# First block of a streaming-encoder layer: x's rows for the norm are loaded two steps sooner into their own memory, and the products of the first weights change order

## The chip, the cores and the metric

The kernel runs on one NeuronCore of a Trainium2 chip. The time is device microseconds of one execution. The runs of the kernel before took 1817.17, 1819.08 and 1819.1 us, median 1819.08 us.

The engines have short names here: PE is TensorE (matmuls; PEld its weight loads), DVE is VectorE, ACT is ScalarE, POOL is GpSimd, and SP is SyncE, which here only issues DMAs. Each engine works through its instructions in order and waits on semaphores.

## The reference, cut to what matters

One layer of an encoder on 256 rows of 2048 numbers: half a gated feed-forward block, a mixer (a state-space part S5 beside attention), a second half feed-forward block, and a gated embedding. The change touches the first feed-forward block and moves preparation of S5 that runs beside it.

```python
x = x + 0.5 * swiglu(rms_norm(x, ffn1_norm[i]), ffn1_w_gate[i], ffn1_w_up[i], ffn1_w_down[i])

def rms_norm(x, gain):
    y = x * lax.rsqrt(jnp.mean(x * x, axis=-1, keepdims=True) + EPS)
    return y * gain

def swiglu(h, w_gate, w_up, w_down):
    return (jax.nn.silu(h @ w_gate) * (h @ w_up)) @ w_down
```

## The kernel before, in words

**Products.** Every matrix product of float32 is split in three: a tensor is cast to a high part (`whi`, `nhi`) by ACT (L181 for weights, L281 or L193 for x), and DVE subtracts that from the source to get the low part (`wlo`, `nlo`; L184, L286, L195). PE adds up high x high (L344), low input x high weight (L345) and high input x low weight (L338). For PE the stationary side is the input and the moving side the weight, 512 columns wide.

**Tiling.** The 256 rows are two tiles of 128 (`t` = 0, 1). The hidden width is cut into blocks of 512 columns (`f`). For each block `gemm_block` (L352) runs over the 2048 input columns in four quarters of 512; a quarter is one DMA of 1 MB into a raw weight buffer (`raw`, five of them, L327 and L328), and is worked in two halves, each 12 matmuls: 2 input rows of 128, 2 row tiles, 3 products. A half is called a half step here; after each, `step()` advances all generators that run beside (`put_off(n, fn)` runs `fn` after n more of these steps). There are four pairs of `whi` and `wlo`, so a cast waits until PE has released the pair four half steps back. The first three blocks of the first feed-forward block take their gate and up products with `gemm_block`, first gate (8 half steps), then up (8 half steps).

**First block.** The first two quarters of the gate product (`first_quarters`, L255) come in small pieces so that PE can start early: four pieces `in_head` that hold x's first columns beside the weights, then x's next columns (`in_turned`) and weights of the second quarter. The inputs are multiplied by the norm's gain but not by the root: since the root is one number per row, it is applied later, at the silu (L720, `scale=xn.rs(t)`) and where gate and up meet (L741). It is computed from sums of squares of x's rows (`squares`, L445 to L453; ACT squares a 128 x 512 piece and sums along the row, L447), from rows that are loaded for this alone (`load_x`, L155 to L157, eight DMAs of 0.26 MB). In the kernel before these rows lie in two of the five raw weight buffers, which `place_x` (L141) takes for the whole of x from the start.

**Accumulators.** Four PSUM banks of 512 columns (`acc`). Gate of a block takes two, up two. The gate product of the second block therefore needs the banks of the first block's gate product, and can start only once the silu has read them.

**Order.** The program is written in steps, but the framework orders the instructions of each engine by its own planning, except where `pin` or `tc.issue_after(ins)` fixes a place. All loads of weights, of x and of the preparation's constants stand in SP's one queue. A DMA there waits for the landing of the DMA eight before it, and for the release of its buffer.

**Beside it** runs the preparation of S5 (`s5_prep`, L834): many small operations of DVE, constants made by ACT, and tables that go to DRAM and back (`rot`, written at L993; `bc` and `bt`, loaded at L1011 and L1012; `coef`, loaded by POOL at L1016). `bc` is used by ACT at L1038 and by DVE at L1032. The finished hidden blocks are turned by DVE (L218), two at a time, and moved into place by small DMAs (`hT`, L231).

Of the kernel before, what the change touches and what calls it, by code (L numbers as in the profile page):

```python
# [9 lines left out]
F32 = mybir.dt.float32  # L10
# [6 lines left out]
P = 128  # L17
# [16 lines left out]
def layer_kernel(ctx: ExitStack, tc: tile.TileContext, a: dict, shapes: dict, out: bass.AP):  # L34
# [60 lines left out]
    def start(g):  # L95
        beside.append(g)
        return g
# [30 lines left out]
    def make_masks():  # L128


        u = com("h")[:, :P]
        nc.sync.dma_start(u, a["not_ahead"])
        nc.scalar.activation(tri_r, u, AF.Copy, scale=-1.0)
        nc.scalar.activation(late_r, u, AF.Copy, scale=-(2.0 ** 100))
        nc.scalar.copy(ident_r, ident)
        nc.scalar.activation(all_r, ones, AF.Copy, scale=-1.0)


    xt = [[], []]
# [1 line left out]
    def place_x():  # L141
        for t in range(TT):
            x = wp.tile([P, ND, NB], F32, tag="raw", name=uid("x"), bufs=5)
            xt[t][:] = [x[:, n, :] for n in range(ND)]
# [4 lines left out]
            for t in range(TT):  # L149
                nc.gpsimd.dma_start(xt[t][n], rows[t * P : (t + 1) * P, n * NB : (n + 1) * NB])  # L150

    place_x()
    scr_x = dramp.tile([T, D], F32, name="scr_x")

    def load_x(n):  # L155
        for t in range(TT):
            nc.sync.dma_start(xt[t][n], a["x"][0, t * P : (t + 1) * P, n * NB : (n + 1) * NB])  # L157

    def load_turned(n):
# [13 lines left out]
        return gains[:, c0 + k : c0 + k + n]  # L173


    rests = []

    def split(hi, lo, src, scale=None, pinned=False):

        if scale is None:  # L180
            copy = nc.scalar.copy(hi, src)  # L181
            if pinned:
                pin(copy)
            rest = nc.vector.tensor_tensor(out=lo, in0=src, in1=hi.bitcast(F32), op=ALU.subtract)  # L184
            rests.append(rest.ins)
            return copy.ins, rest.ins
        else:
            split_each(hi.unsqueeze(1), lo.unsqueeze(1), src.unsqueeze(1), [scale])
# [142 lines left out]
    def gemm_half(ps, half, ts, start, stop, cols=slice(0, NB), in_turn=False):  # L331

        (ahi, alo), (h, hi, lo) = half

        def rest(j):
            for t in ts:
                lh = ahi[:, 2 * h + j, t * P : (t + 1) * P]
                nc.tensor.matmul(ps[t], lhsT=lh, rhs=lo[:, j, cols], start=False, stop=stop and j == 1)  # L338

        for j in range(2):  # L340
            for t in ts:
                lh = ahi[:, 2 * h + j, t * P : (t + 1) * P]
                ll = alo[:, 2 * h + j, t * P : (t + 1) * P]
                nc.tensor.matmul(ps[t], lhsT=lh, rhs=hi[:, j, cols], start=start and j == 0, stop=False)  # L344
                nc.tensor.matmul(ps[t], lhsT=ll, rhs=hi[:, j, cols], start=False, stop=False)  # L345
            if in_turn:
                rest(j)
        if not in_turn:
            for j in range(2):
                rest(j)  # L350
# [275 lines left out]
    def ffn(i, xn, nxt, bg=None):  # L626
# [26 lines left out]
        for f in range(NF):  # L653
# [69 lines left out]
            if f == 0:  # L723
                warm_up(8)
                first = first_quarters(wg, xn)
                put_off(6, next, prep)
            pg = gemm_block(xn, wg, f * NB, KD, first)
            sg = com("sg")
            if f == 0:
                for n in range(ND):  # L730
                    put_off(n, load_x, n)
                    put_off(n + 2, xn.squares, n)
                put_off(6, gate)
            else:
                gate()
            pu = gemm_block(xn, wu, f * NB, KD)
            if prep and f == 0:
                start(prep)
            hh = com("h")
            for t in range(TT):  # L740
# [93 lines left out]
    def s5_prep(pools):  # L834
        base = pools.enter_context(phase("prep"))
        par = get(base, "par", 3 * NR)
        nc.sync.dma_start(par, a["ssm_par"])
        yield
        make_masks()
# [985 lines left out]
```

## Time and profile before

| what | us |
|---|---|
| median of three runs | 1819.08 |
| the profiled execution | 1819.03 |
| its span, from the first to the last instruction | 1817.1 |
| PE busy in the span | 1807.7 |
| DVE busy | 1574.8 |
| ACT busy | 1065.7 |
| POOL busy | 104.5 |
| PE busy in the first 140 us | 135.55 |
| DVE busy in the first 140 us | 119.28 |

The span is read from the profiled execution; the 1.9 us beside it are the execution's time ahead of and behind the first and the last instruction. A row of a timeline reads: start in us from the span's start, duration, engine, line, operation, what it writes and reads, count; behind it in brackets how long the engine had stood idle and what ended the wait. A row of a windows view reads: the stretch, its length, then the busy time and number of instructions that PE, PEld, DVE, ACT and POOL have in it, the mean granted clock of PE as a share of full speed, the share of the DMA engines' time, and GB/s. Busy PE time counts matmuls that overlap as one.

### The profile page before, as it was taken

To read this page: it belongs to the slowest core of one execution; us is meant where nothing else is said; L and a number is where in the kernel's file an instruction comes from. 1 tells how busy PE (TensorE), PEld (TensorE's weight loads), DVE (VectorE), ACT (ScalarE), POOL (GpSimd) and SP (SyncE) were. 2 spreads that over 40 slices of the span, in tenths; PEclk is the share of its full clock that TensorE was granted. 3 is DMA by queue.
4 is the path that set the end of the run, shared out by engine and by line. 5 is a ranking of instruction groups with operands and counts; after the bars stand their busy time and mean duration, and the time that the engine had idled before them with its cause. 6 is when DMAs were issued, how large, how long until landed. Compare 5 with 4: busy or idle time off the path is not lost.

```text
span 1817.1 us, 24209 instructions
## 1 busy us (share of the span) xinstructions
PE 1807.7 (99%) x8914; PEld 1498.9 (82%) x8914; DVE 1574.8 (87%) x1840; ACT 1065.7 (59%) x1240; POOL 104.5 (6%) x160
## 2 busy tenths in 40 slices
PE   9999999999999999999999999999999999999998
PEld 7788888888888888888898888888888888888887
DVE  8978889999998896687567899999999999889875
ACT  7445456655565665365685566555565556566654
POOL 0020100000000001110021000000000010000000
PEclk9999999999999999999999999999999999999999
DMA  8699877677876667674636787777767786666663
GB/s 331 262 270 315 246 247 232 232 251 235 264 248 229 198 232 251 192 255 163 220 129 218 237 299 218 265 261 249 233 231 235 242 276 239 224 208 221 201 245 128
DMA packets 107799, 428.41 MB, mean 236 GB/s; under 512 B 24512, under 2 KB 48352, under 8 KB 65280
## 3 DMA queue, kind: packets, MB, share of 16 engines
q1 hardware_dynamic: 96832, 391.15, 61.2%
q0 software_dynamic: 10560, 35.40, 9.0%
q8 instruction: 70, 1.15, 0.2%
q14 instruction: 49, 0.40, 0.1%
q10 hardware_dynamic: 288, 0.31, 0.1%
HBM read 372.41 MB, written 10.88 MB: 211 GB/s over the span
## 4 chain that ended last, share of the span: by engine, by line
PE 95%; DVE 1%; DMA 0%; issue 0%; ACT 0%; DVEq 0%; ACTq 0%
PE acc L344 16%; PE acc L345 16%; PE acc L338 15%; PE aux L345 7%; PE aux L344 7%; PE aux L338 7%; PE acc L526 5%; PE acc L529 5%; PE acc L527 5%; PE aux L527 3%; PE aux L529 3%; PE aux L526 3%; PE aux L1233 0%; PE acc L1484 0%; PE acc L1489 0%; PE acc L1480 0%
## 5 line engine op out<-in xcount | busy, mean ns | idle before, releaser
L184 DVE TENSOR_TENSOR wlo<-raw,whi 128x1024 fp32r<-128x1024 f32 x478 | 578.8, 1224 | 127.4 <-ACT whi L181 122.0
L181 ACT CAST whi<-raw 128x1024 fp32r<-128x1024 f32 x478 | 496.1, 1050 | 297.7 <-PE acc L345 183.7
L344 PE MATMUL acc<-whi,nhi 128*128 128x512 f32 x908 | 357.5, 394 | 3.4 <-ACT sg L720 2.3
L345 PE MATMUL acc<-whi,nlo 128*128 128x512 f32 x908 | 355.0, 391 | 0.0
L338 PE MATMUL acc<-wlo,nhi 128*128 128x512 f32 x908 | 253.2, 390 | 0.1
L184 DVE TENSOR_TENSOR slo<-raw,shi 128x1024 fp32r<-128x1024 f32 x186 | 226.6, 1218 | 16.0 <-ACT shi L181 15.2
L181 ACT CAST shi<-raw 128x1024 fp32r<-128x1024 f32 x186 | 195.2, 1050 | 65.3 <-DMA raw<-in_ffn_w_down 22.2
L344 PEld LDWEIGHTS acc<-whi,nhi 128*128 128x128 f32 x908 | 171.2, 189 | 41.2 <-ACT sg L720 2.7
L338 PEld LDWEIGHTS acc<-wlo,nhi 128*128 128x128 f32 x908 | 170.8, 188 | 36.0 <-DVE wlo L184 0.5
L345 PEld LDWEIGHTS acc<-whi,nlo 128*128 128x128 f32 x908 | 171.3, 189 | 34.6
L181 ACT CAST whi<-sum 128x1024 fp32r<-128x1024 f32 x79 | 83.3, 1054 | 157.5 <-DVE sum L533 138.4
L181 ACT CAST shi<-sum 128x1024 fp32r<-128x1024 f32 x59 | 62.2, 1054 | 101.6 <-DVE sum L533 96.1
L533 DVE TENSOR_TENSOR sum<-sum,raw 128x1024 f32<-128x1024 f32 x92 | 112.3, 1221 | 0.9
L184 DVE TENSOR_TENSOR wlo<-sum,whi 128x1024 fp32r<-128x1024 f32 x79 | 96.4, 1222 | 5.0 <-ACT whi L181 4.3
L594 POOL DMA_DIRECT2D raw<-raw x44 | 38.2, 868 | 1031.8 <-DVE sum L533 697.4
L344 PE MATMUL aux<-whi,nhi 128*128 128x512 f32 x220 | 85.8, 390 | 0.0
L345 PE MATMUL aux<-whi,nlo 128*128 128x512 f32 x220 | 85.7, 390 | 0.0
L184 DVE TENSOR_TENSOR slo<-sum,shi 128x1024 fp32r<-128x1024 f32 x59 | 72.1, 1222 | 1.1 <-ACT shi L181 0.5
L338 PE MATMUL aux<-wlo,nhi 128*128 128x512 f32 x220 | 67.8, 390 | 0.0
L533 DVE TENSOR_TENSOR sum<-raw,raw 128x1024 f32<-128x1024 f32 x46 | 56.1, 1220 | 7.2 <-DMA raw<-in_ffn_w_up 3.5
L345 PE MATMUL acc<-whi,hlo 128*128 128x512 f32 x156 | 60.8, 390 | 0.0
L344 PE MATMUL acc<-whi,hhi 128*128 128x512 f32 x156 | 60.7, 389 | 0.0
(393 smaller groups left out, 3410.3 us busy)
## 6 DMA issues: line engine op xcount, KB each, us to landing
raw<-in_ffn_w_up SPq DMA_DIRECT2D x88, 1024.0 KB, 5.7
raw<-in_ffn_w_down SPq DMA_DIRECT2D x88, 1024.0 KB, 4.9
raw<-in_ffn_w_gate SPq DMA_DIRECT2D x86, 1024.0 KB, 7.0
raw<-in_w_in SPq DMA_DIRECT2D x32, 1024.0 KB, 5.1
raw<-raw POOLq DMA_DIRECT2D x46, 512.0 KB, 5.5
raw<-in_w_out SPq DMA_DIRECT2D x16, 1024.0 KB, 4.9
raw<-in_w_ple_gate SPq DMA_DIRECT2D x16, 1024.0 KB, 5.1
hT<-mid SPq DMA_DIRECT2D x160, 64.0 KB, 4.7
```

Of the source, the lines that this page charges most:

```text
L181: copy = nc.scalar.copy(hi, src)
L184: rest = nc.vector.tensor_tensor(out=lo, in0=src, in1=hi.bitcast(F32), op=ALU.subtract)
L338: nc.tensor.matmul(ps[t], lhsT=lh, rhs=lo[:, j, cols], start=False, stop=stop and j == 1)
L344: nc.tensor.matmul(ps[t], lhsT=lh, rhs=hi[:, j, cols], start=start and j == 0, stop=False)
L345: nc.tensor.matmul(ps[t], lhsT=ll, rhs=hi[:, j, cols], start=False, stop=False)
L526: nc.tensor.matmul(ps, lhsT=lh[j], rhs=hi[:, j], start=begin and j == 0, stop=False)
L527: nc.tensor.matmul(ps, lhsT=ll[j], rhs=hi[:, j], start=False, stop=False)
L529: nc.tensor.matmul(ps, lhsT=lh[j], rhs=lo[:, j], start=False, stop=z in final and j == 1)
L533: nc.vector.tensor_tensor(out=t, in0=x, in1=y, op=ALU.add)
L594: nc.gpsimd.dma_start(b12, b22, accum_op=ALU.add)
```

## The change

The diff in full:

```diff
@@ make_masks @@
-        nc.scalar.copy(ident_r, ident)
-        nc.scalar.activation(all_r, ones, AF.Copy, scale=-1.0)
+        with tc.issue_after(copies[9]):
+            nc.scalar.copy(ident_r, ident)
+            nc.scalar.activation(all_r, ones, AF.Copy, scale=-1.0)
@@ layer_kernel @@
-    place_x()
     scr_x = dramp.tile([T, D], F32, name="scr_x")
 
-    def load_x(n):
+    def load_x(pool, n):
         for t in range(TT):
+            xt[t].append(pool.tile([P, NB], F32, name=uid("row")))
             nc.sync.dma_start(xt[t][n], a["x"][0, t * P : (t + 1) * P, n * NB : (n + 1) * NB])
@@ split @@
-    rests = []
+    rests, copies = [], []
...
             rests.append(rest.ins)
+            copies.append(copy.ins)
             return copy.ins, rest.ins
@@ gemm_half @@
         for j in range(2):
-            for t in ts:
-                lh = ahi[:, 2 * h + j, t * P : (t + 1) * P]
-                ll = alo[:, 2 * h + j, t * P : (t + 1) * P]
-                nc.tensor.matmul(ps[t], lhsT=lh, rhs=hi[:, j, cols], start=start and j == 0, stop=False)
-                nc.tensor.matmul(ps[t], lhsT=ll, rhs=hi[:, j, cols], start=False, stop=False)
+            products = [(t, i) for t in ts for i in range(2)]
+            for t, i in sorted(products, key=lambda p: p[::-1]) if in_turn else products:
+                nc.tensor.matmul(
+                    ps[t], lhsT=(ahi, alo)[i][:, 2 * h + j, t * P : (t + 1) * P], rhs=hi[:, j, cols],
+                    start=start and j == 0 and i == 0, stop=False,
+                )
@@ ffn @@
             if f == 0:
                 warm_up(8)
                 first = first_quarters(wg, xn)
+                next(prep)
+                side_rows = ExitStack()
+                pool = side_rows.enter_context(phase("rows"))
+                for n in range(ND):
+                    put_off(n + 6, load_x, pool, n)
+                    put_off(n + 8, xn.squares, n)
                 put_off(6, next, prep)
             pg = gemm_block(xn, wg, f * NB, KD, first)
             sg = com("sg")
             if f == 0:
-                for n in range(ND):
-                    put_off(n, load_x, n)
-                    put_off(n + 2, xn.squares, n)
-                put_off(6, gate)
+                put_off(4, gate)
             else:
                 gate()
             pu = gemm_block(xn, wu, f * NB, KD)
             if prep and f == 0:
+                side_rows.close()
                 start(prep)
@@ s5_prep @@
         par = get(base, "par", 3 * NR)
+        yield
         nc.sync.dma_start(par, a["ssm_par"])
```

The loads of x's rows and their squares are counted from the start of the gate product instead of its end: n + 6 of its eight half steps instead of n after them, two steps sooner each. The gate's silu is put off by 4 steps of the up product instead of 6. The rows get eight tiles of a pool of their own, which is closed when the first block is done, so that the preparation's later tiles lie on the same memory. The five raw buffers are all left to weights until x is fetched for good behind the hidden blocks. `par` is allocated ahead of that pool. In the first quarter alone (`in_turn`) the two high x high products of the two row tiles now come ahead of the two with the low input. Two constants that ACT makes for the attention (`ident_r`, `all_r`) are held back behind a later weight cast.

Since lines are added, a line of the kernel after stands one to eight further down than its counterpart before: L158 is L157, L182 is L181, L330 is L328, L450 is L447, L723 is L720.

**SP's queue, from the gate weights' last quarter on.** `raw` are weights, `x` or `row` are x's rows, `par` a constant of the preparation. Before:

```order
L328 DMA raw_292<-in_ffn_w_gate 128x2048
L837 DMA par_317<-in_ssm_par 128x96
L328 DMA raw_334<-in_ffn_w_up 128x2048
L157 DMA x_89<-in_x 128x512
L157 DMA x_90<-in_x 128x512
L157 DMA x_89<-in_x 128x512
L157 DMA x_90<-in_x 128x512
L328 DMA raw_372<-in_ffn_w_up 128x2048
```

and after:

```order
L330 DMA raw_297<-in_ffn_w_gate 128x2048
L158 DMA row_319<-in_x 128x512
L158 DMA row_321<-in_x 128x512
L845 DMA par_185<-in_ssm_par 128x96
L158 DMA row_336<-in_x 128x512
L158 DMA row_338<-in_x 128x512
L330 DMA raw_343<-in_ffn_w_up 128x2048
L158 DMA row_369<-in_x 128x512
L158 DMA row_371<-in_x 128x512
L158 DMA row_389<-in_x 128x512
L158 DMA row_391<-in_x 128x512
L330 DMA raw_393<-in_ffn_w_up 128x2048
```

Four of x's rows have moved ahead of the up weights' first quarter, and the other four ahead of the second.

**ACT, from the last square to the silu of the first block.** `sq` is a square, `whi` a weight cast, `sm` the root, `sg` the silu, `s5s` a sine of the preparation. Before:

```order
L447 ACTIVATE sq_458,sm_110<-x_90 128x512
L181 CAST whi_516<-raw_514 128x1024
L181 CAST whi_520<-raw_514 128x1024
L205 ACT_TABLE_LOAD
L205 ACTIVATE sm_465<-sm_463 128x2
L181 CAST whi_575<-raw_573 128x1024
L181 CAST whi_579<-raw_573 128x1024
L720 ACT_TABLE_LOAD
L720 ACTIVATE sg_331<-acc_184,sm_465 128x512
L720 ACTIVATE sg_331<-acc_185,sm_465 128x512
```

and after:

```order
L182 CAST whi_486<-raw_484 128x1024
L182 CAST whi_490<-raw_484 128x1024
L207 ACT_TABLE_LOAD
L207 ACTIVATE sm_440<-sm_438 128x2
L136 CAST ident_r<-ident 128x128
L137 ACTIVATE all_r<-ones 128x128
L893 ACT_TABLE_LOAD
L893 ACTIVATE s5s_564<-s5s_564 128x32
L182 CAST whi_526<-raw_524 128x1024
L723 ACT_TABLE_LOAD
L723 ACTIVATE sg_340<-acc_189,sm_440 128x512
L723 ACTIVATE sg_340<-acc_190,sm_440 128x512
```

The four casts that stood between the last square and the silu before are those of the second block's first two quarters. After, one cast of the second block (`raw_524`) is left ahead of the silu; `raw_484` is the last quarter of the first block's up weights. The two constants and a sine of the preparation have moved in.

**SP's queue, where the first two hidden blocks are moved into place.** `hT` are the pieces of the turned hidden block, `bc` and `bt` constants of the preparation. Before:

```order
L993 DMA scr_rot_105<-rot_877 256x1x512
L328 DMA raw_1197<-in_ffn_w_up 128x2048
L1011 DMA bc_1270<-in_ssm_bc 128x512
L1012 DMA bt_1271<-in_ssm_b_turned 128x1024
L1011 DMA bc_1589<-in_ssm_bc 128x512
L328 DMA raw_1240<-in_ffn_w_up 128x2048
L231 DMA hT_157_1044<-mid_615 32x2x256 x12
```

and after:

```order
L1001 DMA scr_rot_103<-rot_887 256x1x512
L330 DMA raw_1250<-in_ffn_w_up 128x2048
L233 DMA hT_163_1054<-mid_625 32x2x256 x4
L1019 DMA bc_1280<-in_ssm_bc 128x512
L1020 DMA bt_1281<-in_ssm_b_turned 128x1024
L233 DMA hT_163_1054<-mid_625 32x2x256 x8
L330 DMA raw_1313<-in_ffn_w_up 128x2048
```

`bc` and `bt` now stand behind the first four pieces of `hT`, which wait for DVE's transposes; the write of `rot`, on whose memory `bc` lies, stands one load of weights further back as well.

## The prediction

> **What bounds the kernel now.** I read the page's first part, then its chain of work, to see which engine the time belongs to.
>
> ```profile
> span 1817.1 us, 24209 instructions
> PE 1807.7 (99%) x8914; PEld 1498.9 (82%) x8914; DVE 1574.8 (87%) x1840; ACT 1065.7 (59%) x1240; POOL 104.5 (6%) x160
> PE 95%; DVE 1%; DMA 0%; issue 0%; ACT 0%; DVEq 0%; ACTq 0%
> ```
>
> TensorE (PE) is busy 99% of the span and 95% of the chain. The change removes no matmul, so it can only save time in which PE stands still or runs below its pace. Next come PE's waits in the first 140 us, where the change lies.
>
> ```profile
> PE acc L344 <- ACT sg L720: 2.3, 1, 2.3
> PE aux L250 <- POOL ones L125: 1.1, 1, 1.1
> PE acc L344 <- ACT whi L285: 0.6, 1, 0.6
> PE acc L344 <- ACT whi L295: 0.4, 1, 0.4
> ```
>
> The largest is one wait of the second hidden block's first matmul for the first block's silu (L720, tile sg). ScalarE's (ACT's) timeline shows why the silu is so late, and PE's timeline what stands on both sides of the gap.
>
> ```profile
> 41.30 0.62 ACT L447 ACTIVATE sq<-x 128x512 f32<-128x512 f32 x1
> ...
> 44.51 1.06 ACT L181 CAST whi<-raw 128x1024 fp32r<-128x1024 f32 x1 [1.55 <-PE acc L345]
> 45.59 1.28 ACT L205 ACT_TABLE_LOAD   x1
> 46.88 0.20 ACT L205 ACTIVATE sm<-sm 128x2 f32<-128x2 f32 x1
> 47.23 1.06 ACT L181 CAST whi<-raw 128x1024 fp32r<-128x1024 f32 x1
> 50.01 1.05 ACT L181 CAST whi<-raw 128x1024 fp32r<-128x1024 f32 x1 [1.72 <-PE acc L345]
> 51.07 1.28 ACT L720 ACT_TABLE_LOAD   x1
> 52.37 1.26 ACT L720 ACTIVATE sg<-acc,sm 128x512 f32<-128x512 f32 x2
> ...
> 49.75 1.07 PE L338 MATMUL acc<-wlo,nhi 128*128 128x512 f32 x4
> 53.10 0.50 PE L344 MATMUL acc<-whi,nhi 128*128 128x512 f32 x1 [2.29 <-ACT sg L720]
> ```
>
> The last square of x's rows runs at 41.30, and only then can the root follow. Two more casts, each waiting for PE to free a weight buffer, stand ahead of the silu in ACT's order. PE needs the accumulator banks that the silu reads, so it stops. The windows of this place show what it costs.
>
> ```profile
> 50.66:53.10 2.44, 0.16 (x1) 0.00 (x0) 1.99 (x10) 2.41 (x4) 0.00 (x0) 1.00 1.03 420
> 53.10:57.55 4.45, 4.45 (x13) 3.54 (x14) 3.13 (x9) 1.43 (x2) 0.00 (x0) 0.62 1.00 407
> 57.55:60.27 2.72, 2.72 (x13) 2.25 (x12) 2.43 (x11) 0.78 (x2) 0.00 (x0) 1.00 0.05 18
> ```
>
> A half step (two of a quarter's four rows of weights) is 12 matmuls, and a window's count includes one that reaches in from before. The third window is one half step at full pace: 2.72 us, so 0.227 us a matmul. The fourth matmul of the 49.75 row starts at 49.75 + 3 x 0.227 = 50.43, and the next was due at 50.66. It starts at 53.10: **2.44 us lost**. The half step after it takes 4.45 us at a mean granted clock of 0.62, against 2.72: **1.73 us lost**. Together 4.17 us.
>
> **The change, part by part.**
>
> *Squares and silu earlier.* What goes if the silu is early enough is the whole 4.17 us: the wait, and the slow half step behind it. Whether it is early enough I work out along the new order, from where x's rows now land.
>
> ```profile
> 23.30 2.01 ACT L181 CAST whi<-raw 128x1024 fp32r<-128x1024 f32 x2 [0.69 <-DMA raw<-in_ffn_w_up]
> 28.54 2.00 ACT L181 CAST whi<-raw 128x1024 fp32r<-128x1024 f32 x2 [3.23 <-DMA raw<-in_ffn_w_up]
> 30.44 0.63 ACT L447 ACTIVATE sq<-x 128x512 f32<-128x512 f32 x1
> ...
> 31.20 0.63 ACT L447 ACTIVATE sq<-x 128x512 f32<-128x512 f32 x1
> ```
>
> Both casts start as their DMA lands: the up weights' first quarter at 23.2, their second at 28.5. Between them lie 1.05 MB of weights and four of x's rows (0.26 MB each), so 2.1 MB take 5.3 us and four rows about 2.6. The first four rows now stand ahead of the first up quarter, and it lands at about 25.9; the other four stand ahead of the second quarter, which then lands at about 31.1. That is 2.6 later for both. From the third on all eight rows are through either way.
>
> ACT's sum: casts of the first up quarter 25.9 to 27.9; four squares at the 0.76 pitch of the two rows above, to 30.9; casts of the second 31.1 to 33.1; two squares to 34.6; cast, square, cast, square (1.05 + 0.76 each) to 38.2; two casts to 40.3; table load and root (1.28 + 0.20) to 41.8; the two constants that L135 and L136 make, moved here, about 0.6, to 42.4; a table load and one sine, 1.5, to 43.9; the cast of the next block's first half step to 44.95; table load 1.28; two silus 1.26, to **47.5**. PE wants the banks at 50.66, so the silu has 3.2 us to spare, where it was 2.44 late. VectorE's (DVE's) part of the root, small operations of 0.2 us between splits, ends near 44.5 and is covered.
>
> *The up weights 2.6 us later.* This has a price if its cover is gone. The places:
>
> ```profile
> 24.38 2.36 DVE L184 TENSOR_TENSOR wlo<-raw,whi 128x1024 fp32r<-128x1024 f32 x2 [0.31 <-ACT whi L181]
> 26.66 0.17 DVE L854 TENSOR_SCALAR s5s<-par 128x32 f32<-128x32 f32 x1
> ...
> 31.49 1.22 DVE L184 TENSOR_TENSOR wlo<-raw,whi 128x1024 fp32r<-128x1024 f32 x1
> ...
> 28.90 0.39 PE L344 MATMUL acc<-whi,nhi 128*128 128x512 f32 x1
> ...
> 34.34 0.39 PE L344 MATMUL acc<-whi,nhi 128*128 128x512 f32 x1
> ...
> 36.15 1.07 PE L338 MATMUL acc<-wlo,nhi 128*128 128x512 f32 x4
> ```
>
> PE starts the first up quarter at 28.90; its first cast now ends at 26.95, 1.95 ahead. On DVE the two splits run 27.0 to 29.3, then the state-space preparation, whose order there is unchanged, takes the 4.83 from 26.66 to 31.49: to 34.1. The second quarter's first split (1.2) ends at 35.3; PE wants it at 36.15. That leaves 0.8 us: thin, but I take nothing for it. If the DMAs are slower than reckoned, this is what is late, by at most about 1 us.
>
> *Products in another order, constants moved.* Only the first quarter's products change places.
>
> ```profile
> 7.63 0.51 ACT L281 ACTIVATE nhi<-raw,gains 128x256 fp32r<-128x256 f32 x1 [1.67 <-DMA raw<-in_head]
> 8.70 0.50 PE L344 MATMUL acc<-whi,nhi 128*128 128x512 f32 x1 [0.59 <-ACT whi L285]
> ...
> 10.50 0.28 ACT L135 CAST ident_r<-ident 128x128 fp32r<-128x128 f32 x1
> 10.98 1.05 ACT L295 CAST whi<-raw 128x1024 fp32r<-128x1024 f32 x1 [0.20 <-DMA raw<-in_ffn_w_gate]
> ```
>
> What PE gains ahead of 8.70 it then waits away, since the third piece of in_head is what ends that wait. The 0.28 of L135 freed at 10.50 goes the same way: the cast behind it waited for a DMA. These DMAs stand ahead of the rows in the queue and do not move. Between 0 and 0.6 (the wait at 8.70) gained, I take 0, as the DMA rows say.
>
> *Memory of their own.* Five weight buffers instead of three for weights up to about 41 us can only bring weights sooner. The eight rows lie on memory that the preparation takes afterwards; its big tile's write to DRAM moves behind two weight loads, and what that does is the third rival.
>
> **Sum.** Nothing else in the first block changes PE's work: -2.44 - 1.73 = -4.17. The profiled execution took 1819.03 us (span 1817.1 and 1.9 around it), within 0.05 of the median of the runs. 1819.03 - 4.17 = **1814.9**, a span of 1812.9.
>
> **Rivals.** (1) The up weights come too late for PE at 36.15, as priced: 0 to 1 us back, middle 1815.4. For it speaks the margin of 0.8; against it that DMA runs at full share here, steadily.
>
> (2) The clock loss stays. In the windows a gap of 2.44 us was followed by half pace. If that pace had another cause than the gap, only the gap would go: 1819.03 - 2.44 = 1816.6. Or it falls at another gap: with the reordered products the one ahead of 8.70 may grow from 0.6 towards 0.9; with 1.73 lost there and the 0.4 at L295 absorbed, 1814.9 + 1.3 = 1816.2. Against both: the 0.62 stands right behind the gap, and the gaps of 0.6 and 0.4 cost no clock. The Trainium skill ("TensorE: Matmul & The Clock Gate", Part 1) says that the clock halves after at least one idle window of some 3.4 us, and that the windows run free of the kernel. By that rule read strictly 2.44 us is too short to halve it, which is the 1816.6; the row speaks against that reading, and I go by the row.
>
> (3) The preparation's constants come late and DVE stands in front of a split. In the new order of SP's queue the load bc stands behind four hT issues.
>
> ```profile
> 98.81 0.33 SPq L1011 DMA_DIRECT2D bc<-in_ssm_bc  x1
> 102.39 14.30 SPq L231 DMA_DIRECT2D hT<-mid  x12
> 104.30 0.30 ACT L1038 COPY ce<-bc 128x128 f32<-128x128 f32 x1 [5.28 <-DMA bc<-in_ssm_bc]
> 106.73 0.76 DVE L1032 TENSOR_TENSOR t<-bc,s5s 128x256 f32<-128x256 f32 x2
> ...
> DMA to landing us min/median/max: 5.5/7.6/9.0
> ```
>
> Before, ACT waited 5.28 us for bc and PE felt nothing. Now, with the transposes between 98.2 and 102.4 and four issues at 14.30 / 12 = 1.2 each, bc is issued at 103 to 107 and lands, with the median of its own row, at 110.6 to 114.8. DVE needs it ahead of the split of the third block's first up half step. PE starts that at 50.66 + 24 x 2.72 = 115.9 and wants the split 1.81 later, at 117.7. DVE spends 0.76 and about 0.57 on bc's products and 1.22 on the split, so bc must land by 115.2. The longest 9.0 gives 116.2: 1 us back, 1815.9. For the other side, slower: the longest landing of x's rows is 12.2 us.
>
> ```profile
> DMA to landing us min/median/max: 7.2/8.9/12.2
> ```
>
> From 107.2 that is 119.4: PE stops 4.2 us, loses 1.73 to the clock again, and the time is 1820.8. Break-even is a landing at about 117.6. Against it: four of four landings of bc stayed under 9.0.
>
> (4) The change doesn't do what it says: the silu still comes after 50.66, because ACT's sum is short by over 3.2 us. Then part of the gap and the clock loss stay: about 1817.
>
> **How the numbers follow.** Forecast 0.66; rival 1 0.12; rival 2 0.05; rival 3 0.08 for the small case and 0.05 for the slow one; rival 4 0.04. The range reaches from 1813.0 (the forecast less 1.9, by which the fastest run of before lay under its median) to 1817.3 (rival 4 and all but the slow case). A measurement of this kernel can tell some 0.2%, 3.64 us, from no change, so the border is 1815.4, only 0.5 above the forecast: I give four fifths of the forecast's chance and half of rival 1's to faster, 0.59; the slow case to slower, 0.05; the rest, 0.36, to the same.
>
> **What would show it.** Right: no wait of PE for sg near 50.7, granted clock 1.00 through 50 to 60, the silu at about 46 to 47.5, and the first cast of in_ffn_w_up near 25.9. The small rival shows as a PE wait for wlo near 36, the third as ACT or DVE waiting for bc with a PE wait for wlo near 118. Wrong would be a gap at 50.7 that lasts, or any PE gap over 1 us between 60 and 130.

## The result, and the profile after

| | before | after |
|---|---|---|
| median of 18 runs each, us | 1818.01 (1816.47 to 1820.48) | 1814.55 (1813.96 to 1817.37) |
| ratio of after to before | | 0.9983, 95% interval 0.9976 to 0.9991 |
| the profiled execution, us | 1819.03 | 1816.04 |
| its span, us | 1817.1 | 1814.3 |

The medians differ by 3.46 us, and the interval of the ratio allows 1.6 to 4.4. The forecast was 1814.9. By the border that the prediction drew, 3.64 us, a gain of 3.46 is still "the same", to which it gave 0.36, and not "faster", to which it gave 0.59. The first and the fourth part of the page of after stand beside those of before:

```profile
span 1814.3 us, 24211 instructions
PE 1806.9 (100%) x8914; PEld 1497.1 (83%) x8914; DVE 1573.8 (87%) x1840; ACT 1065.2 (59%) x1240; POOL 104.8 (6%) x160
...
PE 96%; DMA 2%; DVE 1%; SPq 1%; ACT 0%; issue 0%; ACTq 0%; DVEq 0%
```

PE does the same 8914 matmuls in a span that is 2.8 us shorter. Its waits in the first 140 us (waiting, times, longest) no longer hold the 2.3 us for the silu; a wait for a wlo is new:

```profile
PE aux L252 <- POOL ones L125: 1.1, 1, 1.1
PE acc L340 <- DVE wlo L185: 0.5, 1, 0.5
PE acc L345 <- ACT whi L297: 0.3, 1, 0.3
```

ACT's timeline of after, from the first cast of the up weights to the silu:

```profile
27.07 2.00 ACT L182 CAST whi<-raw 128x1024 fp32r<-128x1024 f32 x2 [4.79 <-DMA raw<-in_ffn_w_up]
...
38.01 0.63 ACT L450 ACTIVATE sq<-row 128x512 f32<-128x512 f32 x1
...
41.99 0.20 ACT L207 ACTIVATE sm<-sm 128x2 f32<-128x2 f32 x1
...
44.03 1.03 ACT L182 CAST whi<-raw 128x1024 fp32r<-128x1024 f32 x1
45.08 1.28 ACT L723 ACT_TABLE_LOAD   x1
46.37 1.27 ACT L723 ACTIVATE sg<-acc,sm 128x512 f32<-128x512 f32 x2
```

The last square has moved from 41.30 to 38.01, and the silus end at 46.37 + 1.27 = 47.6, where the prediction had 47.5. The windows of three half steps around the place of the old stall:

```profile
48.49:51.21 2.72, 2.72 (x14) 2.25 (x12) 2.56 (x4) 1.81 (x4) 0.00 (x0) 1.00 0.46 101
51.21:53.93 2.72, 2.72 (x14) 2.25 (x12) 2.72 (x17) 1.11 (x2) 0.00 (x0) 1.00 0.84 337
53.93:56.65 2.72, 2.72 (x14) 2.25 (x12) 2.72 (x5) 1.46 (x4) 0.00 (x0) 1.00 0.20 36
```

Each takes 2.72 us, PE is busy throughout, and the granted clock is 1.00. The half step that starts at 53.93 started at 57.55 before: 3.62 us sooner. That is the 4.17 of the sum less 0.55. Where the 0.55 went, the timelines show between 28 and 38 us, DVE's first and then PE's:

```profile
30.43 0.17 DVE L862 TENSOR_SCALAR s5s<-par 128x32 f32<-128x32 f32 x1
...
35.26 2.35 DVE L185 TENSOR_TENSOR wlo<-raw,whi 128x1024 fp32r<-128x1024 f32 x2
```

```profile
28.62 0.39 PE L345 MATMUL acc<-whi,nhi 128*128 128x512 f32 x1
...
36.53 1.21 PE L340 MATMUL acc<-wlo,nhi 128*128 128x512 f32 x4 [0.49 <-DVE wlo L185]
37.58 0.40 PE L345 MATMUL acc<-whi,nhi 128*128 128x512 f32 x1
```

PE came to the up product 0.28 sooner than the 28.90 of before. DVE was in the preparation from 30.43 to 35.26 and began the split for the second up quarter's wlo only then. PE wanted that wlo at 28.62 + 32 x 0.2267 = 35.87 and went on at 36.53; it reached the next half step at 37.58 instead of 35.87 + 4 x 0.2267 = 36.78. So 0.8 us are lost here, 0.66 in the wait and 0.14 in slower starts behind it, and 0.8 less the 0.28 is the 0.55 but for a few hundredths. Of the 3.62, some is given back much later, in a place the change doesn't touch:

```profile
1281.17 0.39 PE L530 MATMUL aux<-shi,nlo 128*128 128x512 f32 x1
1281.91 0.73 PE L532 MATMUL aux<-slo,nhi 128*128 128x512 f32 x2 [0.35 <-DVE slo L185]
```

The second row was due 0.23 behind the first, at 1281.40, so 0.5 us goes there, and slower starts in the next 5 us take another 0.1, in this execution. The rest of the difference between 3.62 and the spans' 2.8, some 0.2 us, is spread over the span.

The third rival's place is quiet. ACT waited 2.03 us for bc and PE for nothing:

```profile
111.00 0.30 ACT L1046 COPY ce<-bc 128x128 f32<-128x128 f32 x1 [2.03 <-DMA bc<-in_ssm_bc]
```

bc was there at 111.00, at the early end of the 110.6 to 114.8 that had been reckoned, and 4 us ahead of the 115.2 by which it was needed.

### The profile page after: what moved, and what is told of

It reads as the page before. It is cut to its first block, busy times and chain, and to the rows that moved or that the text cites. A ratio compares the mean times of both kernels' runs of the same rounds, so it can differ in the third digit from the quotient of the medians.

```text
span 1814.3 us, 24211 instructions
## 1 busy us (share of the span) xinstructions
PE 1806.9 (100%) x8914; PEld 1497.1 (83%) x8914; DVE 1573.8 (87%) x1840; ACT 1065.2 (59%) x1240; POOL 104.8 (6%) x160
## 4 chain that ended last, share of the span: by engine, by line
PE 96%; DMA 2%; DVE 1%; SPq 1%; ACT 0%; issue 0%; ACTq 0%; DVEq 0%
PE acc L345 32%; PE acc L340 16%; PE aux L345 15%; PE aux L340 7%; PE acc L529 5%; PE acc L532 5%; PE acc L530 5%; PE aux L532 3%; PE aux L530 3%; PE aux L529 3%; DMA raw<-in_ffn_w_up 1%; SPq L233 0%; DMA sg<-in_turned 0%; PE aux L1241 0%; PE acc L1497 0%; PE acc L1492 0%
## 5 line engine op out<-in xcount | busy, mean ns | idle before, releaser
L182 ACT CAST whi<-raw 128x1024 fp32r<-128x1024 f32 x478 | 496.3, 1050 | 295.5 <-PE acc L345 182.7
L182 ACT CAST shi<-raw 128x1024 fp32r<-128x1024 f32 x186 | 195.1, 1049 | 61.4 <-DMA raw<-in_ffn_w_down 22.3
L182 ACT CAST whi<-sum 128x1024 fp32r<-128x1024 f32 x79 | 83.3, 1054 | 160.1 <-DVE sum L536 143.9
L182 ACT CAST shi<-sum 128x1024 fp32r<-128x1024 f32 x59 | 62.2, 1054 | 101.8 <-DVE sum L536 91.5
```

## The experiments

Medians of 10 or 11 runs each; before ran beside them each time, with medians of 1817.48 to 1818.19.

| run | what it is | median (lowest to highest), us | ratio to before, 95% interval |
|---|---|---|---|
| e0_after_again | after, once more | 1814.58 (1813.51 to 1815.93) | 0.9982 [0.9974, 0.9991] |
| e1_order_only | before + new order of products | 1817.45 (1815.86 to 1818.64) | 0.9998 [0.999, 1.0007] |
| e2_no_order | after with the old order of products | 1814.24 (1813.5 to 1814.97) | 0.9981 [0.9972, 0.999] |
| e3_old_steps | after with the step numbers of before | 1813.98 (1813.56 to 1814.46) | 0.9978 [0.9969, 0.9987] |
| b_const | before + the constants held back | 1814.24 (1813.36 to 1814.96) | 0.9981 [0.9973, 0.999] |
| b_mem | before + memory for the rows | 1817.98 (1816.33 to 1819.32) | 0.9998 [0.9989, 1.0007] |
| b_steps | before + the new step numbers | 1814.54 (1814.03 to 1815.91) | 0.9982 [0.9973, 0.9991] |
| e5_prep_later | after + the preparation later | 1813.83 (1813.44 to 1815.51) | 0.9979 [0.9971, 0.9988] |
| e7_gap_short | after + silu five times (one tile) | 1814.86 (1814.35 to 1815.24) | 0.9981 [0.9973, 0.999] |
| e7_gap_long | after + silu eight times (one tile) | 1816.09 (1815.32 to 1816.94) | 0.9988 [0.9979, 0.9997] |
| e8_before_again | before, once more | 1817.5 (1816.63 to 1818.96) | 0.9997 [0.9988, 1.0006] |
| e10_gap_5us | after + both silus eight times | 1821.31 (1820.11 to 1822.2) | 1.0019 [1.0009, 1.0028] |

### Which part of the change makes the gain?

**The old steps in the new kernel.** The first test was meant to confirm that the sooner squares make the gain.

```diff
-                    put_off(n + 6, load_x, pool, n)
-                    put_off(n + 8, xn.squares, n)
+                    put_off(n + 8, load_x, pool, n)
+                    put_off(n + 10, xn.squares, n)
...
-                put_off(4, gate)
+                put_off(6, gate)
```

> The changed kernel with the three step numbers of before (loads n + 8, squares n + 10, silu put off by 6) but the rows still in memory of their own. Theory A: the steps make the gain: the last square falls at 40 to 41 again, the root and the silu behind it, PE waits for the silu near 50.5 for 2 to 3 us, the granted clock falls to about 0.6 in the half step behind it, and the time is 1818 to 1819. Rival B: the memory makes it, since five raw buffers let the up weights' later quarters come sooner: the silu is ready before 50.5 and the time is 1814 to 1815.

The theory fell: 1813.98, with the squares as late as before. ACT's timeline of this run shows how that can be:

```profile
41.55 0.63 ACT L450 ACTIVATE sq<-row 128x512 f32<-128x512 f32 x1
...
44.41 1.06 ACT L182 CAST whi<-raw 128x1024 fp32r<-128x1024 f32 x1 [1.20 <-PE acc L345]
...
46.78 0.20 ACT L207 ACTIVATE sm<-sm 128x2 f32<-128x2 f32 x1
...
47.13 1.05 ACT L182 CAST whi<-raw 128x1024 fp32r<-128x1024 f32 x1
48.20 1.28 ACT L723 ACT_TABLE_LOAD   x1
49.50 1.27 ACT L723 ACTIVATE sg<-acc,sm 128x512 f32<-128x512 f32 x2
50.66 1.05 ACT L182 CAST whi<-raw 128x1024 fp32r<-128x1024 f32 x1
```

The last square is at 41.55, later than the 41.30 of before, and the root at 46.78 instead of 46.88. But the silu starts at 49.50 instead of 52.37. Before, two casts stood between the root and the silu, and the second waited 1.72 us for PE, at 50.01. Here one of them stands behind the silu (50.66). That suffices. In this kernel memory, constants and products are all still those of after. Each was tried alone on the kernel before.

**The products alone.** The edit is the change's own, in `gemm_half`.

> The kernel before with nothing but the new order of the first quarter's products. Theory A: PE comes to the up product 0.28 us sooner (28.62 instead of 28.90), as it did in the changed kernel, but the silu ends at 52.4 + 0.7 as before, since ACT's work does not depend on PE there; so the wait for the silu grows from 2.44 to about 2.7 us, PE starts the second block at 53.1 as before, and the time is that of before within 0.5 us. Rival B: the 0.28 us is carried to the end: PE starts the second block at 52.8 and the time is about 0.3 us below that of before.

The time is that of before (0.9998). The window from the start of the last matmul ahead of the wait to the first behind it:

```profile
49.84:52.51 2.67, 0.39 (x2) 0.00 (x0) 2.56 (x14) 2.64 (x4) 0.00 (x0) 1.00 1.04 427
```

Theory A had the wait grow by 0.28 us; it did not. PE came to it 0.59 us sooner than before (49.84 for 50.43) and went on 0.59 us sooner (52.51 for 53.10), 2.67 us from start to start both times, which is the 2.44 lost and one matmul's 0.23. So over these 0.59 us the length of the wait does not depend on when PE arrives. It is a chain that PE itself starts: the cast ahead of the silu waits for PE to release a weight pair near the end of the first block, and behind it come a table load and the silu. This profile says nothing on whether the new order makes PE earlier, since with the old order PE's place moves by nearly as much from one execution to the next (50.43 in before, 49.97 in e8_before_again, below).

**The old products in the new kernel.**

> The changed kernel with the products of the first quarter in the old order. PE comes to the up product at 28.90 instead of 28.62. Theory A: where the second up quarter's wlo is late, the wait near 36 is 0.28 us shorter and all that follows stands as in the changed kernel (second block at 51.2): the order gains nothing; median 1814.6. Rival B: the wlo is in time in most executions and the order is worth 0.28 us to the end: median 1814.8 and the second block at 50.7. Rival C: the order matters for more than that (a longer wait ahead of 8.7 with its clock loss): 1816 or more.

1814.24 against 1814.55 and 1814.58 of after: the order of the products gains nothing that these runs can tell. In its profile PE waited 0.31 us for the late wlo near 36, so A's mechanism was there.

**The memory alone.**

```diff
-    place_x()
...
-    def load_x(n):
+    def load_x(pool, n):
         for t in range(TT):
+            xt[t].append(pool.tile([P, NB], F32, name=uid("row")))
...
```

The lines left out open and close the pool of the rows and allocate `par` ahead of it, as in the change.

> The kernel before with the rows in memory of their own and nothing else changed; ACT's order is that of before. Theory A: memory gives nothing by itself, since the casts ahead of the silu wait for PE and not for a DMA: the wait for the silu stays at 2.3 us, the half step behind it at a clock near 0.6, the time 1817.5 to 1818.5, though the second block's gate weights land sooner (near 41 instead of 45.6). Rival B: the sooner weights bring the casts and the silu forward, 1814 to 1815.

Nothing: 1817.98. ACT's timeline has the cast ahead of the silu waiting for PE and for no weights, as before:

```profile
49.54 1.05 ACT L181 CAST whi<-raw 128x1024 fp32r<-128x1024 f32 x1 [1.72 <-PE acc L345]
50.61 1.28 ACT L720 ACT_TABLE_LOAD   x1
51.91 1.26 ACT L720 ACTIVATE sg<-acc,sm 128x512 f32<-128x512 f32 x2
```

**The constants alone.** This is the edit for which the prediction took 0.

```diff
-        nc.scalar.copy(ident_r, ident)
-        nc.scalar.activation(all_r, ones, AF.Copy, scale=-1.0)
+        with tc.issue_after(copies[9]):
+            nc.scalar.copy(ident_r, ident)
+            nc.scalar.activation(all_r, ones, AF.Copy, scale=-1.0)
...
```

> The kernel before with one edit of the change alone: the two constants for the attention held back behind a later cast (issue_after), which I had priced at nothing. x's rows, squares, silu steps, memory and products are as before. In ACT's order this alone leaves one cast of the second block less ahead of the silu, the one that waited 1.72 us for PE at 50.01. Theory A (the silu was late because of that cast as much as because of the squares): root done at 47.1, the constant 0.3, cast to 48.4, table load to 49.7, first silu to 50.3, which is ahead of 50.66; PE does not wait, the clock does not fall, and the time is 1814 to 1814.5. Rival B (my prediction's step: the squares' move makes the gain): the wait of 2.3 us and the half pace behind it stay, 1817.5 to 1818.5.

This alone gives the whole gain: 1814.24, ratio 0.9981. ACT's order from the root on, before and with this edit (`raw_514` and `raw_573` are the second block's first two quarters):

```
before                                    constants held back
L205 ACTIVATE sm_465<-sm_463              L207 ACTIVATE sm_465<-sm_463
                                          L137 ACTIVATE all_r<-ones
L181 CAST whi_575<-raw_573                L182 CAST whi_575<-raw_573
L181 CAST whi_579<-raw_573
L720 ACT_TABLE_LOAD                       L722 ACT_TABLE_LOAD
L720 ACTIVATE sg_331<-acc_184,sm_465      L722 ACTIVATE sg_331<-acc_184,sm_465
L720 ACTIVATE sg_331<-acc_185,sm_465      L722 ACTIVATE sg_331<-acc_185,sm_465
                                          L182 CAST whi_579<-raw_573
```

ACT's timeline of this run, with the last square where it was, and the windows of the last half step ahead of the old stall and the first one behind it:

```profile
41.51 0.62 ACT L449 ACTIVATE sq<-x 128x512 f32<-128x512 f32 x1
...
47.00 0.20 ACT L207 ACTIVATE sm<-sm 128x2 f32<-128x2 f32 x1
47.11 0.29 ACT L137 ACTIVATE all_r<-ones 128x128 fp32r<-128x128 f32 x1
47.35 1.06 ACT L182 CAST whi<-raw 128x1024 fp32r<-128x1024 f32 x1
48.43 1.28 ACT L722 ACT_TABLE_LOAD   x1
49.72 1.27 ACT L722 ACTIVATE sg<-acc,sm 128x512 f32<-128x512 f32 x2
50.88 1.05 ACT L182 CAST whi<-raw 128x1024 fp32r<-128x1024 f32 x1
```

```profile
48.06:50.78 2.72, 2.72 (x13) 2.25 (x12) 2.72 (x20) 2.69 (x4) 0.00 (x0) 1.00 1.02 422
50.78:53.50 2.72, 2.72 (x13) 2.25 (x12) 2.69 (x10) 1.81 (x3) 0.00 (x0) 1.00 1.02 428
```

The first silu is done by 50.4, and PE takes the bank at 50.78 without a pause. PE had 0.4 us to spare. Why the planner turns the silu and the cast around when a 0.3 us constant comes between, these runs do not show; that it does is plain from the order.

**The steps alone.** The rows are in the raw buffers, and products and constants are as before.

```diff
+                for n in range(ND):
+                    put_off(n + 6, load_x, n)
+                    put_off(n + 8, xn.squares, n)
                 put_off(6, next, prep)
...
-                for n in range(ND):
-                    put_off(n, load_x, n)
-                    put_off(n + 2, xn.squares, n)
-                put_off(6, gate)
+                put_off(4, gate)
```

> The kernel before with the steps alone: loads at n + 6, squares at n + 8, silu put off by 4; rows in the raw buffers, products and constants as before. Theory A (two edits of the change each remove the stall): silu done at 47 to 47.5 as in the changed kernel, no wait near 50.7; the up weights land 2.6 to 3.9 us later, so PE waits 0 to 0.7 us for a wlo near 36, and the time is 1814 to 1815.5. Rival B (the steps need the memory of their own): the rows hold two raw buffers, the up product's third and fourth quarter come late and PE waits for them between 39 and 48 by more than 1 us, 1816 or more.

Theory A: 1814.54. Here too the silu stands ahead of the cast that waits for PE:

```profile
44.92 1.27 ACT L720 ACTIVATE sg<-acc,sm 128x512 f32<-128x512 f32 x2
...
49.48 1.05 ACT L181 CAST whi<-raw 128x1024 fp32r<-128x1024 f32 x1 [1.28 <-PE acc L345]
```

So two parts of the change, the constants and the steps, each remove the stall without the other, and in both the waiting cast ends up behind the silu. In this run the root is sooner as well, at 40.92; b_const and e3_old_steps show that this is not needed. Sooner squares with that cast still ahead of the silu were not tried. The other two parts, the memory and the products, gain nothing that can be measured.

### What the early rows cost, and whether that sets the spread

> The changed kernel once more. Its 18 runs fell into two groups, 13 of 1814.0 to 1814.9 us and 5 of 1816.0 to 1817.4, and the profiled one (1816.04) is of the slower group; in it the first up quarter landed at 26.97 instead of the 25.9 that I had reckoned, and PE waited at 35.9 for a wlo (0.65 us, and 0.15 of half pace behind it) and once more near 1281 (0.5 us). Theory A: the late landing is a matter of the single execution; a profile from the faster group has the landing near 25.9, no wait near 36, and a span near 1812.4. Theory B: the wait near 36 is in every execution, since the landing at 27 follows from the queue's order; then a profile of the faster group shows it too, and the 2 us between the groups lie elsewhere, near 1281 or where a third engine is late. Either way the silu ends at 47 to 48 and PE does not wait for it.

Of A, the late landing is a matter of the execution: here the first cast of the up weights starts at 26.18, and PE waits for no wlo near 36.

```profile
26.18 2.00 ACT L182 CAST whi<-raw 128x1024 fp32r<-128x1024 f32 x2 [4.06 <-DMA raw<-in_ffn_w_up]
```

But this profiled execution took 1815.34, in the upper half of its runs, with another wait far behind, at 1674.94 (of the waits view: waiting, times, longest):

```profile
PE acc L345 <- DVE hlo L185: 0.6, 1, 0.6
```

So an execution can be among the slower ones without the wait near 36. The second test of this holds back the start of the preparation on DVE until the second up quarter's split instead of the first's:

```diff
-        with tc.issue_after(rests[5]):
+        with tc.issue_after(rests[6]):
             exp(dt, ldt)
...
-        with tc.issue_after(rests[5]):
+        with tc.issue_after(rests[6]):
             ts(lr, lr, LAMBDA_RE_MAX, None, op0=ALU.min)
```

> The changed kernel with the first 4.8 us of the preparation on DVE held back behind the split of the second up quarter instead of the first. Theory A (what the early rows cost is the wait near 36, made by DVE's preparation between the two quarters' splits): wlo is ready about 2 us ahead of PE in every execution, no wait near 36, and the runs lie at 1813.5 to 1814.5, without the group at 1815 to 1817. Rival B: the wait is not what sets the two groups apart, and the runs spread as in the changed kernel, median 1814.6. Rival C: the preparation ends later, bc's products come late and PE waits near 118: 1816 or more.

In its profile the only wait of PE that the view lists is the one for `ones`, ahead of the first product, although the first cast started at 26.50. The median is 1813.83, 0.7 below that of after, with a ratio whose interval overlaps that of after widely. Three of its eleven runs still lay at 1815.3 to 1815.5. So A is right on the wait near 36 and wrong on the spread. What makes a late product near 1281 or 1675 in some executions stays open; no run here was aimed at it. No run of e2_no_order, e3_old_steps or b_const lay above 1815, and e2_no_order has the early rows, which speaks against the early rows alone as the cause of the spread. The fastest two kernels are this one and e3_old_steps, whose up weights are not delayed at all; neither can be told from after.

### The clock behind a wait

The 1.73 us of the sum that belong to the half pace were taken from one execution. The profile of b_mem had the same wait of 2.44 us (its windows: the last matmul ahead of the wait to the first behind it, then 4.9 us):

```profile
49.97:52.64 2.67, 0.38 (x2) 0.00 (x0) 2.17 (x11) 2.64 (x4) 0.00 (x0) 1.00 0.43 178
52.64:57.55 4.91, 4.91 (x22) 4.07 (x23) 4.79 (x15) 1.58 (x2) 0.00 (x0) 1.00 0.61 217
```

22 matmuls start or run in 4.9 us, at a clock of 1.00: no half pace. Four runs follow this up. First, before once more:

> The kernel before once more. Theory A (the wait for the silu of about 2.44 us is in every execution, the half pace behind it in only about half of them, as the profile of the kernel with the rows in memory of their own had the wait and a clock of 1.00): the runs spread from 1816.3 to 1819.5, and the profile shows the wait of 2.3 us; if its time is below 1817 the clock behind the wait is 1.00, if above 1818.5 near 0.6. Rival B: the clock loss is in every execution and the spread has another place: a profile below 1817 that shows the half pace all the same.

Its profiled execution took 1816.82. Its windows, cut in the same way:

```profile
49.97:52.64 2.67, 0.39 (x2) 0.00 (x1) 2.64 (x15) 2.64 (x4) 0.00 (x0) 1.00 0.98 412
52.64:57.55 4.91, 4.91 (x22) 4.05 (x23) 4.82 (x16) 1.58 (x2) 0.00 (x0) 1.00 1.03 407
```

Theory A: the wait again, to the hundredth of a microsecond, and no loss of clock behind it. In the profile of e1_order_only, which took 1818.64, the loss is there:

```profile
52.51:57.38 4.87, 4.87 (x14) 3.83 (x15) 3.69 (x10) 1.58 (x2) 0.00 (x0) 0.66 1.01 404
```

So the same program text around the same wait has the half pace in two profiles (1819.03 and 1818.64 us) and not in two others (1816.74 and 1816.82). For other lengths of the wait, the silu was repeated:

```diff
             def gate():
                 for t in range(TT):
-                    nc.scalar.activation(sg[:, t * NB : (t + 1) * NB], pg[t], AF.Silu, scale=xn.rs(t))
+                    for _ in range(5 if f == t == 0 else 1):
+                        nc.scalar.activation(sg[:, t * NB : (t + 1) * NB], pg[t], AF.Silu, scale=xn.rs(t))
```

> The changed kernel with the first row tile's silu of the first block computed five times instead of once (the same values again), to open PE's wait there on purpose. By the changed kernel's rows the fifth ends at about 52.4, and PE wants the bank at 50.4 to 51.2: a wait of 1.2 to 2.0 us. Theory A (whether the clock falls after a wait depends on how the wait lies to something that runs free of the kernel, so a shorter wait is hit more rarely than the 2.44 us of before, which is hit in about half of the executions): clock 1.00 behind the wait in most executions, median 1814.5 + 1.6 = 1816.1, a minority 1.7 higher. Rival B (every wait over some 1 us is followed by the half pace, so that the wait of 2.44 us costs 1.73 more each time): 1817.5 to 1818 in all runs, clock near 0.62 in the half step behind.

> The same with eight times: the eighth ends at about 55.4, a wait of 4.2 to 5.0 us. Theory A: a wait this long is hit in nearly every execution, median 1814.5 + 4.6 + 1.7 = 1820.8 with little spread. Rival B: the same 1.7 of clock as for 2.44 us, 1820.8 too; the two are told apart by the short wait. Rival C (the half pace has nothing to do with the wait): clock 1.00 behind it in most executions, median 1819.1.

Both missed their lengths: ACT ran 0.6 us ahead of the reckoning, casts came between the repeated silus, and in the longer one PE waited not for the repeated silu but for the product of gate and up (L749). PE lost 0.4 and 1.3 us there. The windows of the longer one:

```profile
51.74:53.03 1.29, 0.15 (x1) 0.00 (x0) 1.29 (x7) 1.26 (x3) 0.00 (x0) 1.00 1.02 432
53.03:55.87 2.84, 2.84 (x12) 2.36 (x13) 2.84 (x4) 2.26 (x3) 0.00 (x0) 1.00 0.54 176
```

A wait of 1.3 us was followed by 2.84 us for 12 matmuls and a clock of 1.00. The median, 1816.09, is close to the 1814.6 + 1.3 that the wait alone explains and leaves no room for 1.7 more in most runs. Five of the eleven lie at 1816.5 to 1816.9; whether the clock fell in any of these, no profile shows. With both silus eight times:

> The changed kernel with both silus of the first block computed eight times (the same values again), ACT's order otherwise as it was there. Sixteen at 0.61 from 45.8 on: the first row tile's last ends near 55.0, and PE wants the bank at 50.4 to 50.8: a wait of 4.2 to 4.7 us. Theory A (the half pace needs a wait that covers a stretch of a clock that runs free of the kernel; waits of 2.45 us cover it in some executions, of 1.3 us in none that was seen): a wait this long is followed by the half pace in every execution; granted clock near 0.6 in the half step behind, median 1814.5 + 4.5 + 1.7 = 1820.7. Rival B (the half pace is a matter of chance whatever the wait): a median of 1819.0 to 1819.9 with runs on both sides. Rival C (no clock loss at all here): 1819.0, clock 1.00.

```profile
49.99:54.01 4.02, 0.16 (x2) 0.01 (x1) 0.02 (x1) 4.02 (x8) 0.00 (x0) 0.87 0.00 0
54.01:59.29 5.28, 5.28 (x12) 4.12 (x13) 5.28 (x6) 4.86 (x8) 0.00 (x0) 0.50 0.20 47
```

The wait is 4.0 us, the clock falls while PE still waits (0.87), and the 12 matmuls behind it take 5.28 instead of 2.72, at 0.50 throughout. The median, 1821.31, is 2.8 us above after's 1814.55 plus the 4.0 of the wait, and the lowest run 1.6 above: theory A, with a larger loss than expected. That truly every run lost to the clock is not shown, since a few of after's own runs lie 1.5 us above their median.

The trace's record of the clock says when it fell. The stretches at half clock in before, e1_order_only and e10_gap_5us are these:

```profile
53.50:56.91 3.41, 3.41 (x10) 2.67 (x9) 2.73 (x7) 0.39 (x2) 0.00 (x0) 0.50 1.02 413
54.04:57.46 3.42, 3.42 (x10) 2.64 (x9) 2.24 (x6) 1.04 (x1) 0.00 (x0) 0.50 1.01 398
52.97:59.80 6.83, 5.79 (x14) 4.54 (x15) 5.81 (x7) 5.90 (x10) 0.00 (x0) 0.50 0.22 65
```

The record has the clock first at its full share at 5.71, 6.26 and 5.18 us, and in all three it fell 47.79 us later. That is 14 times 3.413 us; the three stretches are one, one and two times that. Where nothing was lost, the next change comes only at the kernel's end, 530 (b_mem) and 529 times (e8_before_again) 3.413 us behind the first full share. So in these traces the clock changes on a grid of 3.413 us that starts at another place in each execution, and one step of it at half pace costs half, 1.7 us. In before the clock fell 0.40 us after PE had gone on, in e1_order_only 1.53 us after. In e10_gap_5us 5.79 us of PE's work lie at half pace, which costs 2.9, near the 2.8 above. How much of the wait lies in one step does not decide alone: it is at most 2.44 us in before and 1.88 in e1_order_only, which lost, and 2.01 in b_mem and 1.65 in e8_before_again, which did not. What decides stays open.

## Why the prediction was right, and where it was not

- **PE is the bound, and only the stall and the clock can be saved.** Right: beside the stall and the clock, PE's rows of after show only the 0.8 us near 36 and the 0.6 near 1281.
- **The silu is done at 47.5 in the changed kernel.** Right: 47.6. The parts of ACT's sum erred in both directions. The up weights came at 27.07 for the 25.9 reckoned, but a cast with a square behind it took 1.56 us (35.51 to 37.07 on ACT) instead of 1.81.
- **"The last square of x's rows runs at 41.30, and only then can the root follow."** The root does follow the square, but that is not the cause of the stall, and this step failed. In e3_old_steps and b_const the last square is at 41.5 and the silu still starts at 49.5 and 49.7. The prediction's own rows had it: the root was done at 47.08, and what then held the silu was the cast at 50.01 with its 1.72 us of idle time, waiting for PE. Between the root and the silu of before stand two casts (2.1 us), that wait and a table load (1.28). The prediction names these casts, but says that each waits for PE; of the two behind the root only the one at 50.01 has such a wait in its row. Its ACT sum has one cast ahead of the silu, as the new order does, so the time came out right while the gain was put down to the squares.
- **"Products in another order, constants moved ... I take 0."** Right for the products. For the constants the price of their own work was right, but not what else their move does: alone, it turns the silu ahead of the waiting cast and gives the whole gain. The total came out because in the changed kernel the steps do the same and nothing is added twice.
- **The memory is worth nothing by itself.** Right: 1817.98.
- **2.44 us for the wait.** Right: it is 2.44 us in each of the four profiles with ACT's old order (before, e8_before_again, b_mem, e1_order_only), since PE's own release starts the chain.
- **1.73 us for the clock.** Mis-sized as a term of the median. It was in the profiled execution of before, which lay 1.0 us above the median of 18 runs, but the half pace was absent from two of four profiles with this wait. The second rival, that the loss stays behind the change, did not come true; what did is that the loss was not always there to be saved. Half of 1.73 is about the size of the difference between the 4.17 of the sum and the 3.46 of the medians; it was not measured apart from the smaller terms. That the forecast lies only 0.35 us from the median is in part luck: it starts at 1819.03, 1.0 us above the later median of before, and takes off 0.7 us more than was gained, and the two errors nearly cancel.
- **The first rival (up weights late for PE at 36.15, 0 to 1 us).** It happened in some executions: 0.8 us in the profile of after, next to nothing in that of e0_after_again. Where it happens it eats the 0.28 us by which PE came sooner. That these are due to the products is not shown: with the old order PE reached the up product at 28.90 in before and at 28.43 in e8_before_again.
- **The third rival (bc late).** Did not happen; the margin was 4 us. **The fourth** did not either.

## What to carry to other kernels

Between the event that looks late and the wait that it seems to cause, read each row's idle time: a row that waits for the very engine that is stalled closes a circle. Here an instruction turned around in it was worth the whole gain, and work done sooner was not needed. Where a planner sets the order, price a moved instruction by the order that results and not by its own duration, and test the parts of a change one by one, since two of them can each do the whole. A loss that is read from one profiled execution, above all one of clock, is a term for that execution; look for it in a second one before it goes into a sum for the median.

## What the hardware did that was not expected

The granted clock is not a function of the length of the wait alone. Behind 2.44 us it fell to 0.50 in two profiles of four, behind 1.3 us it did not fall in the one profile, and behind 4.0 us it fell during the wait and stayed at 0.50 for the 5.28 us after it. In the profiles named above every change lies a whole number of times 3.413 us behind the first full share. The Trainium skill ("TensorE: Matmul & The Clock Gate", Part 1) describes an activity window of about 3.4 us that runs free of the kernel, with the slow state after at least one idle window. The grid of 3.413 us that starts at another place in each execution agrees with this. That a wait of 2.44 us, shorter than such a window, was hit at all differs from the rule as it is written, and here the rows decide.

The first up quarter's landing moves from one execution to the next. Its cast waits for it and starts at 27.07 in the profile of after, at 26.18 in e0_after_again and 26.50 in e5_prep_later, and at 25.90 in e10_gap_5us, where 25.9 had been reckoned from the pace of the DMAs in before. So the reckoned time is the early end of what these profiles show. What makes the difference was not tried.
